# Constants of the mixers prepared earlier, the norms' power on two other engines, spare chunks in order, and other waits of query projections

## The chip, the cores and the metric

The kernel runs on one core of a Trainium2 chip. The metric is device time in microseconds (us) of one execution; lower is better. Of several executions the median counts.

## The reference: what is computed

A stack of nine sublayers works on 256 positions of width 1024 in fp32: two layers of a gated feed-forward, a mixer and another gated feed-forward (the first layer's mixer is HGRN2, a linear recurrence in chunks of 64; the second's is FOX, attention with forget gates), and then a block whose three sublayers have norms shifted, scaled and gated by a vector that is computed from a second input `c`. Its mixer, the token mixer, runs a stick-breaking attention with 8 heads and a differential attention with 4, and merges both with gates. Every mixer and feed-forward is a product with large weights (2816 columns in the feed-forward).

```python
def rmsnorm(x, g):
    x32 = x.astype(jnp.float32)
    y = x32 * lax.rsqrt(jnp.mean(x32 * x32, axis=-1, keepdims=True) + EPS)
    return (y * g.astype(jnp.float32)).astype(x.dtype)

def swiglu(h, w_in, w_out):
    gate, up = jnp.split(h @ w_in, 2, axis=-1)
    return (jax.nn.silu(gate) * up) @ w_out
...
    for layer in range(DEPTH):
        x = x + 0.5 * swiglu(rmsnorm(x, norm_g[layer, 0]), ffn_w_in[layer, 0], ffn_w_out[layer, 0])
        hn = rmsnorm(x, norm_g[layer, 1])
        if layer % N_MIXERS == 0:
            x = x + hgrn2_mixer(hn, hg_w_in[j], lbs[j], hg_out_norm_g[j], hg_w_out[j])
        else:
            x = x + fox_mixer(hn, fox_w_in[j], fox_b_f[j], fox_q_norm_g[j], fox_k_norm_g[j], fox_w_out[j])
        x = x + 0.5 * swiglu(rmsnorm(x, norm_g[layer, 2]), ffn_w_in[layer, 1], ffn_w_out[layer, 1])
...
        def sublayer(h, i, fn, resid_w):
            shift = mod[:, i, 0, None, :]
            scale = mod[:, i, 1, None, :]
            gate = mod[:, i, 2, None, :]
            u = rms_norm(h, norm_pre[l, i]) * (1.0 + scale) + shift
            return h + resid_w * gate * rms_norm(fn(u), norm_post[l, i])
...
```

## The kernel before

**Tiling.** The 256 positions are two tiles of 128, t=0 and t=1, which stay in memory on the chip as `X`. Every product is a matmul of fp32 numbers in three parts: `split` (L170 and L171) makes a high part (`H`, `w`, `uh`; a cast on ScalarE, ACT) and a low part (`L`, `q`, `ul`; a subtraction on VectorE, DVE), and `mm3` (L210 to L214) issues high times high, high times low and low times high on TensorE (PE). Weights come in chunks of 512 KB through `loadw` (L173) into 5 buffers `raw`, one DMA each or two, issued by the SyncE queue (SP); each chunk is split into two halves. `H` and `L` have 6 buffers. The next chunk's DMA starts when a `raw` buffer's last low half is made; the next casts into `H` start when PE has read the old ones.

**Stages.** Nine stages run one after another: feed-forward, HGRN2, feed-forward; feed-forward, FOX, feed-forward; ffn1, token mixer, ffn2 (the modulated three). A feed-forward projects gate and up, applies silu on ACT (L559) and a product on DVE (L564), and streams its output weights in `out_stream` (L488). There the last chunks are done first for t=0, then for t=1; what comes after t=0 (`finish`: the update of `X`, then the next stage's `norm` and its eight transposes `T`, L244) is put between the last matmuls of t=1. For t=1 the same is held as `pending` and stands in `first_pair` (L444) of the next stage: PE projects t=0 with the first weight and most of the second, then transposes t=1's norm. Some chunks are spare ones, whose parts go to buffers `w` and `q` of other pools (L188): in the modulated stages two of the output weights' last eight, and the second half of the weight that the next stage projects t=0 with last.

**Norms.** `norm` (L262) squares and sums on ACT (L271), takes mean to the power -1/2 in `rstd2` (L331: an addition on GpSimd, POOL, L333, then `pow`, L335) and scales on DVE (L277 for plain norms; for modulated ones a product with the gain in advance, L273, and then L279). `post_norm` (L348) does the same to the output of each modulated stage (L357, L360) and adds the result to `X` (L362).

**Mixers.** Each starts with constants: masks, gains and biases, loaded by DMAs on POOL's queue and prepared on DVE (HGRN2 from L613, FOX from L763 with DVE's L769 and L771, the token mixer from L971 with L985 and L987). ACT needs a table of functions per kind: silu is in one, ln and exp in another; `lnexp` (L586) loads the latter ahead of a mixer.

**Order.** PE runs in the order that the code is written in. For the mixers `weave` interleaves jobs of heads with projections: a "need" in the stream holds the projections until the named heads are done (token mixer, L1192 and L1203: the differential queries of group g wait for the stick-breaking head 3 of group g). The order of DVE, ACT, POOL and SP is made at compile time by a scheduler that estimates times; each engine then runs its list in that order. `issue_after` bounds what it may put ahead of what. So a row that waits on DVE or ACT holds all rows behind it.

Of the kernel before, what the change touches and what calls it, by code (L numbers as in the profile page):

```python
# [26 lines left out]
D = 1024  # L27
FF = 2816
P = 128
# [51 lines left out]
class Program:  # L81
# [91 lines left out]
    def loadw(self, views, shape, spare=False):  # L173
# [19 lines left out]
        for (h, l), c in zip(halves, parts):  # L193
            self.last_low = self.split(h, l, raw[c])[1]
# [67 lines left out]
    def norm(self, t, gain, shift=None):  # L262
# [11 lines left out]
        r = self.rstd2(s2)  # L274
# [62 lines left out]

    def residual(self, weight):
# [9 lines left out]
    def post_norm(self, tiles):  # L348

        def finish(t, Y):  # L350
# [137 lines left out]
    def out_stream(self, hT, w, nk, finish, last, need=None):  # L488
# [23 lines left out]

        k = 0
# [18 lines left out]
    def ffn(self, wg, wu, wo, finish):  # L532
# [22 lines left out]
        before = None  # L555
        for c0, n in SLICES:
# [23 lines left out]
            before = (c0, n)  # L580
        for n, item in enumerate(self.out_stream(lambda t, k: where[t, k], wo, FF // P, finish, self.lead)):
# [3 lines left out]

    def lnexp(self):  # L586

        es = contextlib.ExitStack()
        with contextlib.ExitStack() as a:
            if self.last_silu is not None:  # L590
                a.enter_context(self.tc.issue_after(self.last_silu.ins))
            pre = self.nc.scalar.preload_act_table_set("natural_log_exp_and_others")
        es.enter_context(self.tc.issue_after(pre.ins))
        return es
# [15 lines left out]
    def hgrn2(self, w, gain, w_out, finish):  # L610
        nc, p = self.nc, self.p

        U = self.tm([9 * P], F32R)  # L613
        raw = self.tm([9 * P])
        nc.gpsimd.dma_start(raw, p["consts"][:, C_U:C_LM])
        nc.vector.tensor_copy(U, raw)
        cm = self.tm([7 * 64 + P + 1])
        nc.gpsimd.dma_start(cm[:, :448], p["consts"][:, C_LM:C_LM + 448])
        nc.gpsimd.dma_start(cm[:, 448:576], p["consts"][:, C_WIDE:C_WIDE + P])
        nc.gpsimd.dma_start(cm[:, 576:], gain.rearrange("o d -> d o"))  # L620
# [140 lines left out]
    def fox(self, w, bf, qg, kg, w_out, finish):  # L761
        nc, p = self.nc, self.p
        cm = self.tm([256 + 16 + 2 + 1])  # L763
        nc.gpsimd.dma_start(cm[:, :272], p["consts"][:, C_FOXM:C_FOXM + 272])
        mask, gains, bias = cm[:, :256], cm[:, 272:274], cm[:, 274:275]
        for j in range(2):
            nc.gpsimd.dma_start(gains[64 * j:64 * j + 64, 0:1], qg.rearrange("o d -> d o"))
            nc.gpsimd.dma_start(gains[64 * j:64 * j + 64, 1:2], kg.rearrange("o d -> d o"))
        nc.vector.tensor_scalar(gains[:, 0:1], gains[:, 0:1], 0.125, None, op0=ALU.mult)  # L769
        sel = self.sm.tile([P, 16], F32R, name="sel", tag="sel", bufs=1)  # L770
        nc.vector.tensor_copy(sel, cm[:, 256:272])  # L771
        for j in range(3):
            nc.gpsimd.dma_start(bias[16 * j:16 * j + 16], bf.rearrange("o h -> h o"))
        zraw = self.t1([8, 16])
        nc.gpsimd.dma_start(zraw, w[:, 4 * D:].rearrange("(k p) f -> p k f", p=P))
        zw = [self.t2([8, 48], F32R) for _ in range(2)]
        self.split(*[x.rearrange("p k (j h) -> p k j h", j=3) for x in zw], zraw[:, :, None, :].to_broadcast([P, 8, 3, 16]))
# [190 lines left out]
    def token_mixer(self, lambda_init, finish):  # L968
        nc, p = self.nc, self.p
        w = p["w_in_2"][0]  # L970
        cm = self.tm([384 + 128 + 128 + 128 + 128])  # L971
        nc.gpsimd.dma_start(cm[:, :640], p["consts"][:, C_DIST:C_DIST + 640])
# [343 lines left out]
```

## Time and profile before

| | |
|---|---|
| runs | 1682.34, 1688.43 and 1692.21 us, median 1688.43 |
| profiled execution | 1683.55 us, its span 1681.7 us |
| PE busy | 1656.0 us (98% of the span), 7862 matmuls |
| DVE, ACT, POOL busy | 1138.4, 905.4 and 121.1 us |
| mean granted PE clock | 0.995 of full speed |
| chain that ended last | PE 79%, issue 11%, DVE 5%, DMA 2% |

PE is the bound nearly everywhere; what a change can move are the few places where PE stands, or runs at the lower clock. Such places are found in the list of PE's waits, in the timelines of the engines and in the tables by stretch, which give each engine's busy time and the clock granted to PE.

### The profile page before, as it was taken

The page shows a single profiled execution, that of the slowest core. Times are in us where ns is not written, and L with a number is a line of the kernel's source. Part 1 is how long each engine was busy: PE and PEld are TensorE (multiplying, and loading weights), DVE is VectorE, ACT ScalarE, POOL GpSimd, SP SyncE. Part 2 cuts the span into 40 slices and gives each one's busy share as a digit, 9 for nine tenths or more (in the row PEclk, how much of TensorE's full clock was granted, in tenths as well). Part 3 has the DMA queues.
Part 4 walks back from the last instruction along what each step waited for, and adds up shares of the span by engine and source line. Part 5 has one row for each costly group of instructions (what it writes and reads, how often), then busy time and mean ns, then how long its engine had stood idle before and what let it go on. Part 6 is the DMA issues. An engine that isn't in the chain of part 4 may idle for free.

```text
span 1681.7 us, 22653 instructions
## 1 busy us (share of the span) xinstructions
PE 1656.0 (98%) x7862; PEld 1370.1 (81%) x7862; DVE 1138.4 (68%) x2015; ACT 905.4 (54%) x1832; POOL 121.1 (7%) x218
## 2 busy tenths in 40 slices
PE   9999999999999999999999999999999999999997
PEld 7888888878888888888888888888887778778886
DVE  6885587867975688656566886575556666775553
ACT  5554476645554555547675554454545658564452
POOL 2000000020000000002211000010002000010000
PEclk9999999999999999999999999999999999999999
DMA  9885553347885588656435896576665525556651
GB/s 325 292 275 193 180 158 99 103 130 237 288 266 186 187 290 279 210 166 190 131 129 168 285 297 216 161 248 187 188 207 173 159 90 167 182 175 177 188 193 57
DMA packets 178132, 329.32 MB, mean 196 GB/s; under 512 B 13665, under 2 KB 66913, under 8 KB 178018
## 3 DMA queue, kind: packets, MB, share of 16 engines
q1 hardware_dynamic: 173328, 318.29, 59.3%
q0 software_dynamic: 4400, 9.06, 1.8%
q8 instruction: 62, 1.02, 0.3%
q10 hardware_dynamic: 290, 0.53, 0.1%
q14 instruction: 52, 0.43, 0.1%
HBM read 326.74 MB, written 1.09 MB: 195 GB/s over the span
## 4 chain that ended last, share of the span: by engine, by line
PE 79%; issue 11%; DVE 5%; DMA 2%; ACT 1%; POOL 1%; SPq 0%; DVEq 0%; POOLq 0%; ACTq 0%
PE acc L212 23%; PE acc L214 23%; PE acc L213 23%; PE T L244 2%; DVE L L171 2%; DMA raw<-in_ffn_w_in 1%; PE T L711 1%; PE acc L680 1%; PE acc L857 1%; ACT H L171 1%; POOL r L333 1%; PE T L956 0%; DVE ad L940 0%; PE T L707 0%; PE T L1063 0%
## 5 line engine op out<-in xcount | busy, mean ns | idle before, releaser
L171 DVE TENSOR_TENSOR L<-raw,H 128x512 fp32r<-128x512 f32 x1044 | 674.9, 687 | 348.6 <-ACT H L171 342.0
L171 ACT CAST H<-raw 128x512 fp32r<-128x512 f32 x1044 | 594.5, 619 | 507.9 <-PE acc L214 352.9
L212 PE MATMUL acc<-H,uh 128*128 128x512 f32 x1456 | 580.5, 399 | 0.2 <-ACT uh L171 0.2
L214 PE MATMUL acc<-H,ul 128*128 128x512 f32 x1456 | 569.1, 391 | 0.3 <-DVE ul L321 0.3
L213 PE MATMUL acc<-L,uh 128*128 128x512 f32 x1456 | 568.7, 391 | 0.0
L214 PEld LDWEIGHTS acc<-H,ul 128*128 128x128 f32 x1456 | 273.9, 188 | 59.7 <-DVE ul L321 1.0
L212 PEld LDWEIGHTS acc<-H,uh 128*128 128x128 f32 x1456 | 274.4, 188 | 54.4 <-issue 0.7
L213 PEld LDWEIGHTS acc<-L,uh 128*128 128x128 f32 x1456 | 274.5, 189 | 52.9
L212 PE MATMUL acc<-H,w 128*128 128x512 f32 x536 | 209.7, 391 | 0.0
L213 PE MATMUL acc<-L,w 128*128 128x512 f32 x536 | 208.6, 389 | 0.0
L214 PE MATMUL acc<-H,q 128*128 128x512 f32 x512 | 199.3, 389 | 0.0
L213 PEld LDWEIGHTS acc<-L,w 128*128 128x128 f32 x536 | 100.7, 188 | 20.6
L212 PEld LDWEIGHTS acc<-H,w 128*128 128x128 f32 x536 | 100.6, 188 | 20.6
L214 PEld LDWEIGHTS acc<-H,q 128*128 128x128 f32 x512 | 96.1, 188 | 19.9
L940 DVE SCALAR_TENSOR_TENSOR ad<-raw,cs,ad 128x512 f32<-128x512 f32 x126 | 94.2, 748 | 2.2
L333 POOL TENSOR_SCALAR r<-s 128x1 f32<-128x1 f32 x24 | 17.5, 728 | 701.5 <-ACT q L357 377.8
L244 PE MATMUL T<-ident,o 128*128 128x128 f32 x400 | 54.2, 276 | 6.3 <-DVE o L277 3.2
L244 PEld LDWEIGHTS T<-ident,o 128*128 128x128 f32 x400 | 46.9, 142 | 15.8 <-issue 7.4
L559 ACT ACTIVATE o<-acc 128x512 f32<-128x512 f32 (+1 forms) x72 | 39.8, 560 | 26.5 <-PE acc L214 26.2
L564 DVE TENSOR_TENSOR o<-o,acc 128x512 f32<-128x512 f32 (+1 forms) x72 | 45.1, 637 | 6.9 <-PE acc L214 4.6
L171 DVE TENSOR_TENSOR q<-T,w 128x512 fp32r<-128x512 f32 (+1 forms) x72 | 43.1, 637 | 0.0
L171 ACT CAST w<-T 128x512 fp32r<-128x512 f32 (+1 forms) x76 | 38.2, 549 | 8.3 <-PE T L244 8.3
(261 smaller groups left out, 1352.6 us busy)
## 6 DMA issues: line engine op xcount, KB each, us to landing
raw<-in_ffn_w_in SPq DMA_DIRECT2D x160, 512.0 KB, 4.9
raw<-in_ffn_w_out SPq DMA_DIRECT2D x88, 512.0 KB, 4.1
raw<-in_w_ada SPq DMA_DIRECT2D x72, 512.0 KB, 4.6
raw<-in_ffn_w_down SPq DMA_DIRECT2D x44, 512.0 KB, 3.3
raw<-in_ffn_w_gate SPq DMA_DIRECT2D x40, 512.0 KB, 3.8
raw<-in_ffn_w_up SPq DMA_DIRECT2D x40, 512.0 KB, 3.8
raw<-in_hg_w_in SPq DMA_DIRECT2D x64, 256.0 KB, 3.7
raw<-in_fox_w_in SPq DMA_DIRECT2D x64, 256.0 KB, 3.6
```

What stands on the lines that cost most here:

```text
L171: return self.nc.scalar.copy(hi, src), self.nc.vector.tensor_sub(lo, src, hi.bitcast(F32))
L212: mm(out, xh, H, start=first, stop=False)
L213: mm(out, xh, L, start=False, stop=False)
L214: mm(out, xl, H, start=False, stop=last)
L244: self.nc.tensor.transpose(T[:, j, :], src[:, (k0 + j) * P:(k0 + j + 1) * P], self.ident)
L333: self.nc.gpsimd.tensor_scalar(r, s2[:, 0:1], s2[:, 1:2], EPS, op0=ALU.add, op1=ALU.add)
L559: self.last_silu = nc.scalar.activation(s[:, :n], A[:, :n], AF.Silu)
L564: nc.vector.tensor_tensor(s[:, :n], s[:, :n], A[:, 512 - n:512], op=ALU.mult)
L680: nc.tensor.matmul(Dp.rearrange("p l c -> p (l c)"), R["lf", t][:, s, h * P:(h + 1) * P], U[:, c0:c0 + 512], start=s == 0, stop=s == 1)
L711: nc.tensor.matmul(SC[n // 3][:, n % 3, h, :].rearrange("p (b s) -> p b s", s=l), EK[h][x0 + 2 + n], q2, start=True, stop=True)
L857: nc.tensor.matmul(S[:, c], R["qz", t][:, h // 2, h % 2, :], kT[:, h // 2, :n], start=True, stop=False)
L940: nc.vector.scalar_tensor_tensor(a, raw[:, k, :], self.cs[:, k0 + k:k0 + k + 1], self.brow0 if k0 + k == 0 else a, op0=ALU.mult, op1=ALU.add)
```

## The change

Six things change.

1. The constants of the three mixers are wrapped in `preparing()`: they may start only after `quiet`, the last power before and the last `up` of the feed-forward that precedes the mixer. In the order they stand at the preceding feed-forward; before, the scheduler put them one stage earlier, next to the norm that ends it.
2. The norms and post-norms issued in the modulated stages take the power in `rstd_act`: an addition on DVE, ln and exp on ACT, and four small operations on DVE (x, and a Newton step). The twelve pairs of POOL operations go.
3. `lnexp` also loads the table of ln and exp in `fetch`, that is at the output weights of ffn1 and ffn2.
4. The spare chunks' splits in `out_stream` are held in the order of the chunks.
5. In the token mixer the differential queries of group 0 need only the start of group 1's stick-breaking, those of group 1 the head 3 of group 0; the gates' first half now needs head 3 of group 1.
6. A parameter for the descriptor memory of POOL's DMAs is set to 8192.

```diff
-            self.last_low = self.split(h, l, raw[c])[1]
+            self.last_split = self.split(h, l, raw[c])
+            self.last_low = self.last_split[1]
...
-        r = self.rstd2(s2)
+        r = self.rstd_act(s2) if self.logs else self.rstd2(s2)
...
+    def rstd_act(self, s2):
+        nc = self.nc
+        a, x, r, t, r2 = [self.ts(1, tag) for tag in ("ra", "rx", "r1", "rt", "rs1")]
+        nc.vector.tensor_scalar(a, s2[:, 0:1], EPS, None, op0=ALU.add)
+        with self.tc.issue_after(self.pre.ins):
+            nc.scalar.activation(r, s2[:, 1:2], AF.Ln, bias=a)
+            nc.scalar.activation(r, r, AF.Exp, scale=-0.5)
+        nc.vector.tensor_tensor(x, s2[:, 1:2], a, op=ALU.add)
+
+        nc.vector.scalar_tensor_tensor(t, r, r, x, op0=ALU.mult, op1=ALU.mult)
+        nc.vector.tensor_scalar(t, t, -0.5, 1.5, op0=ALU.mult, op1=ALU.add)
+        nc.vector.tensor_tensor(r2, t, r, op=ALU.mult)
+        return r2
...
-                    r = self.rstd2(s2)
+                    r = self.rstd_act(s2)
...
-                W[k] = self.loadw([w[k * P:(k + 1) * P, :].rearrange("(k p) f -> p k f", p=P)], [1, D], nk - last <= k < nk - 6)
+                spare = nk - last <= k < nk - 6
+                W[k] = self.loadw([w[k * P:(k + 1) * P, :].rearrange("(k p) f -> p k f", p=P)], [1, D], spare)
+                if spare:
+
+                    for ins in self.last_split:
+                        held.enter_context(self.tc.issue_after(ins.ins))
...
+        held.close()
         after = finish(0, Y[0])
...
+        self.quiet = [self.last_pow.ins]
...
-                nc.vector.tensor_tensor(s[:, :n], s[:, :n], A[:, 512 - n:512], op=ALU.mult)
+                self.last_up = nc.vector.tensor_tensor(s[:, :n], s[:, :n], A[:, 512 - n:512], op=ALU.mult)
...
+        self.quiet.append(self.last_up.ins)
...
+    def preparing(self):
+        es = contextlib.ExitStack()
+        for ins in self.quiet:
+            es.enter_context(self.tc.issue_after(ins))
+        return es
...
+            self.pre = self.nc.scalar.preload_act_table_set("natural_log_exp_and_others")
...
-        cm = self.tm([256 + 16 + 2 + 1])
-        nc.gpsimd.dma_start(cm[:, :272], p["consts"][:, C_FOXM:C_FOXM + 272])
+        with self.preparing():
+            cm = self.tm([256 + 16 + 2 + 1])
+            nc.gpsimd.dma_start(cm[:, :272], p["consts"][:, C_FOXM:C_FOXM + 272])
...
-                yield "need", [("sb", g, 3)]
+                yield "need", [("sb", 0, 3) if g else ("sb", 1)]
...
-                    if hf == 1:
-                        yield "need", [("da", 0, 1)]
+                    yield "need", [("da", 0, 1) if hf else ("sb", 1, 3)]
...
+                if l == 2 and i != 1:
+                    b.lnexp()
...
+            b.logs = l == 2
...
-    nc = _bacc.Bacc("TRN2", target_bir_lowering=False, num_devices=1)
+    nc = _bacc.Bacc("TRN2", target_bir_lowering=False, num_devices=1,
+                    dynamic_dma_scratch_size=8192)
```

**The place of FOX's constants.** POOL, at the end of HGRN2, where t=0's norm for the feed-forward is made (`r_3604`, `rs_3606`), before; `mod` is here the tile of FOX's constants:

```order
L764 DMA mod<-consts 128x272
L767 DMA mod<-in_fox_q_norm_g 64x1
L768 DMA mod<-in_fox_k_norm_g 64x1
L333 TENSOR_SCALAR r_3604<-s_3601 128x1
L767 DMA mod<-in_fox_q_norm_g 64x1
L768 DMA mod<-in_fox_k_norm_g 64x1
L773 DMA mod<-in_fox_b_f 16x1 x3
L335 TENSOR_TENSOR rs_3606<-r_3604,mhalf 128x1
```

And with the change (L334 and L336 are the old L333 and L335, L796 is FOX's first constant, two stages' norms further on):

```order
L334 TENSOR_SCALAR r_3604<-s_3601 128x1
L336 TENSOR_TENSOR rs_3606<-r_3604,mhalf 128x1
...
L334 TENSOR_SCALAR r_5335<-s_5332 128x1
L336 TENSOR_TENSOR rs_5337<-r_5335,mhalf 128x1
L796 DMA mod<-consts 128x272
L799 DMA mod<-in_fox_q_norm_g 64x1
```

The six small DMAs that stood between the addition and the power, or right ahead of them, are gone from there. On DVE at the same place, before:

```order
L171 TENSOR_TENSOR L<-raw,H 128x512 x3
L771 CAST sel<-mod 128x16
L171 TENSOR_TENSOR L<-raw,H 128x512 x3
L769 TENSOR_SCALAR mod<-mod 128x1
L277 SCALAR_TENSOR_TENSOR o_3599<-X_107,rs_3606,mod 128x512
```

And with the change (L278 is the old L277):

```order
L171 TENSOR_TENSOR L<-raw,H 128x512
L278 SCALAR_TENSOR_TENSOR o_3599<-X_107,rs_3606,mod 128x512
L278 SCALAR_TENSOR_TENSOR o_3600<-X_107,rs_3606,mod 128x512
L171 TENSOR_TENSOR L<-raw,H 128x512 x5
```

The norm's product moved ahead of five low halves, and the preparation of FOX's gains (L769) went elsewhere.

**The modulated norm of t=0.** DVE at the end of ffn1, where the token mixer's norm of t=0 is made, before (L273 and L279 are its two products):

```order
L273 TENSOR_TENSOR o_11848<-X_107,mod 128x512
L171 TENSOR_TENSOR L<-raw,H 128x512
L279 SCALAR_TENSOR_TENSOR o_11847<-o_11847,rs_11858,mod 128x512
L279 SCALAR_TENSOR_TENSOR o_11848<-o_11848,rs_11858,mod 128x512
L171 TENSOR_TENSOR L<-raw,H 128x512 x5
```

And with the change (L274 and L280 are the two products; L351 is the Newton step's end):

```order
L274 TENSOR_TENSOR o_11857<-X_107,mod 128x512
L343 TENSOR_SCALAR ra<-s_11858 128x1
L347 TENSOR_TENSOR rx<-s_11858,ra 128x1
L171 TENSOR_TENSOR L<-raw,H 128x512 x4
L349 SCALAR_TENSOR_TENSOR rt<-r_11867,rx 128x1
L171 TENSOR_TENSOR L<-raw,H 128x512
L350 TENSOR_SCALAR rt<-rt 128x1
L171 TENSOR_TENSOR L<-raw,H 128x512
L351 TENSOR_TENSOR rs_11869<-rt,r_11867 128x1
L280 SCALAR_TENSOR_TENSOR o_11856<-o_11856,rs_11869,mod 128x512
L280 SCALAR_TENSOR_TENSOR o_11857<-o_11857,rs_11869,mod 128x512
```

The second product stood behind one low half and stands behind six now; at the end of the token mixer the rows move in the same way.

**The tables.** ACT at the start of ffn2, where t=1's norm is made (`s_13877` its sums, `o_13955` the silu of the first gate), with the change:

```order
L272 ACTIVATE q_13881,s_13877<-X_108 128x512
L583 ACT_TABLE_LOAD
L583 ACTIVATE o_13955<-acc 128x512
L345 ACT_TABLE_LOAD
L345 ACTIVATE r_13886<-s_13877,ra 128x1
L346 ACT_TABLE_LOAD
L346 ACTIVATE r_13886<-r_13886 128x1
L171 CAST uh_114<-T 128x512 x2
```

Before, the load for silu and the silu stood there too; the two loads below and ln and exp are new, and one more load for silu follows.

## Rows read from the trace of the kernel before

**Rows 1.** Page, busy time of each engine, its share of the span and its instructions.
```profile
PE 1656.0 (98%) x7862; PEld 1370.1 (81%) x7862; DVE 1138.4 (68%) x2015; ACT 905.4 (54%) x1832; POOL 121.1 (7%) x218
```

**Rows 2.** PE's waits by line: total us, times, longest us.
```profile
PE T L244 <- DVE o L277: 3.2, 1, 3.2
PE T L244 <- DVE o L279: 2.7, 3, 1.2
PE T L1063 <- DVE w L1059: 2.0, 1, 2.0
PE acc L1093 <- ACT q L1042: 1.9, 2, 1.0
PE acc L213 <- DVE q L171: 1.4, 1, 1.4
```

**Rows 3.** Timeline, HGRN2 to feed-forward: start, us, row, idle before it <-releaser.
```profile
370.07 0.59 POOL L335 TENSOR_TENSOR rs<-r,mhalf 128x1 f32<-128x1 f32 x1
...
371.58 0.15 DVE L769 TENSOR_SCALAR mod<-mod 128x1 f32<-128x1 f32 x1 [1.59 <-DMA mod<-in_fox_q_norm_g]
371.65 1.41 DVE L277 SCALAR_TENSOR_TENSOR o<-X,rs,mod 128x512 f32<-128x512 f32 x2
```

**Rows 4.** By stretch: busy us (x instructions) of each engine, PEclk, DMA share, GB/s.
```profile
372.50:376.50 4.00, 3.96 (x14) 3.51 (x15) 2.60 (x4) 1.17 (x2) 0.00 (x0) 0.50 0.47 173
376.50:380.00 3.50, 3.50 (x13) 2.76 (x12) 2.07 (x4) 3.40 (x8) 0.00 (x0) 0.70 0.01 2
...
1347.00:1349.00 2.00, 2.00 (x9) 1.58 (x8) 1.57 (x4) 1.47 (x3) 0.00 (x0) 0.74 0.75 239
1349.00:1351.00 2.00, 2.00 (x6) 1.61 (x5) 0.70 (x2) 1.54 (x3) 0.00 (x0) 0.50 0.00 1
...
1295.00:1297.00 2.00, 1.74 (x11) 1.48 (x12) 1.24 (x3) 1.03 (x2) 0.86 (x3) 1.00 1.05 350
```

**Rows 5.** Timeline, end of ffn1, the token mixer's norm of t=0.
```profile
1278.12 1.41 DVE L279 SCALAR_TENSOR_TENSOR o<-o,rs,mod 128x512 f32<-128x512 f32 x2
1279.45 3.09 DVE L171 TENSOR_TENSOR L<-raw,H 128x512 fp32r<-128x512 f32 x5
...
1279.86 1.14 ACT L171 CAST H<-raw 128x512 fp32r<-128x512 f32 x2 [0.49 <-ACT H L171]
...
1280.70 1.03 PE L244 MATMUL T<-ident,o 128*128 128x128 f32 x8
```

**Rows 6.** Timeline, start of the token mixer, its norm of t=1.
```profile
1283.19 2.18 ACT L171 CAST H<-raw 128x512 fp32r<-128x512 f32 x4
1285.28 0.59 ACT L357 ACTIVATE q<-acc 128x512 f32<-128x512 f32 x1
...
1286.89 2.18 ACT L171 CAST w<-raw 128x512 fp32r<-128x512 f32 x4
...
1291.00 2.48 DVE L171 TENSOR_TENSOR q<-raw,w 128x512 fp32r<-128x512 f32 x4
1294.33 1.41 DVE L279 SCALAR_TENSOR_TENSOR o<-o,rs,mod 128x512 f32<-128x512 f32 x2 [0.84 <-POOL rs L335]
```

**Rows 7.** Timeline, start of ffn2, its norm of t=1.
```profile
1491.46 1.28 ACT L559 ACT_TABLE_LOAD   x1
1492.76 0.60 ACT L559 ACTIVATE o<-acc 128x512 f32<-128x512 f32 x1
...
1496.04 1.29 PE L244 MATMUL T<-ident,o 128*128 128x128 f32 x8 [1.20 <-DVE o L279]
```

**Rows 8.** By line or tile: ns of one, shortest/median/longest; chunks' DMAs, 1276 to 1290.
```profile
L985 ACT ACTIVATE le<-le x1: 207/207/207, 1214.0 to 1214.0; 128x2 f32<-128x2 f32 x1
...
L987 DVE TENSOR_TENSOR nlam<-le x1: 159/159/159, 1214.3 to 1214.3; 128x1 f32<-128x1 f32 x1
...
L333 POOL TENSOR_SCALAR r<-s x24: 296/352/2926, 5.2 to 1673.2; 128x1 f32<-128x1 f32 x24
...
DMA to landing us min/median/max: 3.0/4.4/5.8
```

More of the change, by code (lines that the diff above doesn't have):

```diff
@@ L611, in hgrn2 @@
         nc, p = self.nc, self.p
[L613 to L620, printed above, removed]
+        with self.preparing():
+            U = self.tm([9 * P], F32R)
+            raw = self.tm([9 * P])
+            nc.gpsimd.dma_start(raw, p["consts"][:, C_U:C_LM])
+            nc.vector.tensor_copy(U, raw)
+            cm = self.tm([7 * 64 + P + 1])
+            nc.gpsimd.dma_start(cm[:, :448], p["consts"][:, C_LM:C_LM + 448])
+            nc.gpsimd.dma_start(cm[:, 448:576], p["consts"][:, C_WIDE:C_WIDE + P])
+            nc.gpsimd.dma_start(cm[:, 576:], gain.rearrange("o d -> d o"))
         lm = cm[:, :448].rearrange("p (l c) -> p l c", l=7).bitcast(U32)
@@ L762, in fox @@
         nc, p = self.nc, self.p
-        cm = self.tm([256 + 16 + 2 + 1])
-        nc.gpsimd.dma_start(cm[:, :272], p["consts"][:, C_FOXM:C_FOXM + 272])
[L765 to L777, printed above, removed]
+        with self.preparing():
+            cm = self.tm([256 + 16 + 2 + 1])
+            nc.gpsimd.dma_start(cm[:, :272], p["consts"][:, C_FOXM:C_FOXM + 272])
+            mask, gains, bias = cm[:, :256], cm[:, 272:274], cm[:, 274:275]
+            for j in range(2):
+                nc.gpsimd.dma_start(gains[64 * j:64 * j + 64, 0:1], qg.rearrange("o d -> d o"))
+                nc.gpsimd.dma_start(gains[64 * j:64 * j + 64, 1:2], kg.rearrange("o d -> d o"))
+            nc.vector.tensor_scalar(gains[:, 0:1], gains[:, 0:1], 0.125, None, op0=ALU.mult)
+            sel = self.sm.tile([P, 16], F32R, name="sel", tag="sel", bufs=1)
+            nc.vector.tensor_copy(sel, cm[:, 256:272])
+            for j in range(3):
+                nc.gpsimd.dma_start(bias[16 * j:16 * j + 16], bf.rearrange("o h -> h o"))
+            zraw = self.t1([8, 16])
+            nc.gpsimd.dma_start(zraw, w[:, 4 * D:].rearrange("(k p) f -> p k f", p=P))
+            zw = [self.t2([8, 48], F32R) for _ in range(2)]
+            self.split(*[x.rearrange("p k (j h) -> p k j h", j=3) for x in zw], zraw[:, :, None, :].to_broadcast([P, 8, 3, 16]))
         cT = self.cT
@@ L981, in token_mixer @@
-        le = self.ts(2, "le")
-        for j in range(2):
-            nc.vector.tensor_tensor_reduce(lv[:, 2 * j, :], lv[:, 2 * j, :], lv[:, 2 * j + 1, :], scale=1.0, scalar=0.0,
-                                           op0=ALU.mult, op1=ALU.add, accum_out=le[:, j:j + 1])
-        nc.scalar.activation(le, le, AF.Exp)
-        nlam = self.ts(1, "nlam")
-        nc.vector.tensor_sub(nlam, le[:, 1:2], le[:, 0:1])
-        nc.vector.tensor_scalar(nlam, nlam, -lambda_init, None, op0=ALU.add)
+        with self.preparing():
+            cm = self.tm([384 + 128 + 128 + 128 + 128])
+            nc.gpsimd.dma_start(cm[:, :640], p["consts"][:, C_DIST:C_DIST + 640])
+            dist, strict, suf, none, sub = cm[:, :384], cm[:, 384:512], cm[:, 512:640], cm[:, 640:768], cm[:, 768:]
+            nc.vector.memset(none, -1.0)
+            nc.gpsimd.dma_start(sub, p["da_subln_2"].to_broadcast([P, P]))
+            nc.vector.tensor_scalar(sub, sub, 1.0 - lambda_init, None, op0=ALU.mult)
+            lv = self.t1([4, 64])
+            for j, name in enumerate(("q1", "k1", "q2", "k2")):
+                nc.gpsimd.dma_start(lv[:, j, :], p[f"da_lambda_{name}_2"].to_broadcast([P, 64]))
+            le = self.ts(2, "le")
+            for j in range(2):
+                nc.vector.tensor_tensor_reduce(lv[:, 2 * j, :], lv[:, 2 * j, :], lv[:, 2 * j + 1, :], scale=1.0, scalar=0.0,
+                                               op0=ALU.mult, op1=ALU.add, accum_out=le[:, j:j + 1])
+            nc.scalar.activation(le, le, AF.Exp)
+            nlam = self.ts(1, "nlam")
+            nc.vector.tensor_sub(nlam, le[:, 1:2], le[:, 0:1])
+            nc.vector.tensor_scalar(nlam, nlam, -lambda_init, None, op0=ALU.add)
@@ L1268, in program @@
                 if i == 1:
-                    with b.lnexp():
+                    with tc.issue_after(b.pre.ins):
                         b.token_mixer(0.8 - 0.6 * math.exp(-0.3 * 0), finish)
@@ L1278, in program @@
                 finish = finisher(b.residual(1.0), following)
-                with b.lnexp():
+                b.lnexp()
+                with tc.issue_after(b.pre.ins):
                     if l == 0:
```

14 lines of the change are left out of this document (1 added, 13 removed).

## The prediction

> **What bounds the kernel now.** PE does: it is busy 1656.0 of 1681.7 us [rows 1], and no edit touches a large matmul. So the change can pay only where PE stands or is granted the lower clock. I read three views for it: the list of PE's waits, whose five main rows make 11.2 us [rows 2]; the timelines of all engines around each of these waits, for what ended last; and the table by stretch, for the clock after the wait. One microsecond of waiting can cost two. After the 3.2 us wait for L277 the clock is 0.50 of full speed (1.2 of 2.4 GHz) for 4.0 us and 0.70 on average for the next 3.5 us; after the 2.0 us wait at L1063 it is 0.74 and 0.50 for 2.0 us each; after a wait of 1.2 us at L279 it stays at 1.00 [rows 4]. So the price behind a long wait is 4.0 x 0.50 + 3.5 x 0.30 = 3.05 us, behind the 2.0 us wait 2.0 x 0.26 + 2.0 x 0.50 = 1.5 us, behind 1.2 us nothing.
>
> **Constants (edit 1).** At the end of HGRN2 the power L335 starts only at 370.07, because FOX's DMAs were ahead of it in POOL's queue; DVE then stands 1.59 us in L769 for one of these DMAs, and the norm's product L277 is queued behind L769, until 371.65 [rows 3]. PE's transposes wait 3.2 us for it [rows 2]. With the change the power follows its addition, and L278 stands behind one low half instead of six and L769. It should be ready before PE asks. Gain: 3.2 + 3.05 = 6.25 us. If another wait of the size of L279's, 1.2 us, shows up in its place, and with it less of the clock, it is 4. The moved work (about ten small DMAs and a few DVE and ACT rows per mixer) now stands behind the last power of a feed-forward, where POOL has nothing urgent queued: POOL is busy 121 us in all [rows 1]. DVE behind a DMA could wait again at the new place, as 1.59 us in L769 [rows 3], but there PE has a whole projection ahead. I take nothing, with 1.5 us as the bound.
>
> **Queries and heads (edit 5).** The waits that this can remove are the 2.0 us at L1063, its clock price 1.5 us, and the 1.9 us at L1093 [rows 2, 4]: 5.4 us. The stretch of heads without projections around 1344 is now filled with projections of the differential queries. But these are taken from later, and a run of heads is left with less filler there; such a run costs from nothing to the 2.0 + 1.5 us that the present one costs. I take a gain of 4.5 us, between 5.4 and a loss of 1.
>
> **Spare chunks (edit 4).** PE waits 1.4 us for `q` of L171 in the output weights of the token mixer [rows 2]. The order of the chunks is now fixed, but the casts and lows before this chunk stay the same in number. I take 0, bounds -1.4 and +0.5 us (a low half more, L171 being 0.62).
>
> **Power on ACT and DVE (edit 2), norm of t=0.** POOL's two operations need 0.30 to 0.35 us (median; once 2.9) and 0.59 [rows 3, 8]. ln and exp together are about 0.4 (L985: 0.207), and a small DVE operation is 0.16 (L987) [rows 8]: an estimate of 0.4 + 0.5 = 0.9 us against 0.9. So by itself the chain costs nothing. What costs is the order. Before, L279 starts at 1278.12, behind one low half, and PE's transposes run at 1280.70 without a wait; the other five lows follow [rows 5]. Now L280 stands behind all six. The last two need casts that don't start before 1279.86, where ACT had idled 0.49 us before them for reasons that the change leaves alone [rows 5]. So: casts until 1281.0, the last low (3.09 / 5 = 0.62) until 1281.6, the end of the Newton step 1281.8, the first product (1.41 / 2) 1282.5. PE wants it at 1280.70: it waits 1.8 us, and 0.2 more for the second product. 2.0 us, and the same at the end of the token mixer.
>
> **Norm of t=1, start of the token mixer.** Before, DVE makes four `q` lows in 2.48 us while POOL does its power, waits 0.84 us for it, and L279 starts at 1294.33, its first half ready at 1295.0 [rows 6]. After, two things come later. First, ACT's list has the casts of the first spare chunk ahead of t=0's `uh` casts and those of the second right behind t=1's first square; before, all four stood behind t=1's squares. The first chunk's DMA can start when the fourth low is done, at about 1280.0, and takes 4.4 us (3.0 to 5.8) [rows 8]: 1284.4. Two casts 1.1 (half of 2.18): 1285.5. The `uh` casts 1.1: 1286.6. A square 0.6: 1287.2. Two spare casts: 1288.3. Then four casts, a square and two casts, which took from 1283.19 to 1286.89, 3.70 us [rows 6]: 1292.0. ln and exp: 1292.4; three small operations of DVE: 1292.9; the two products that make `X` 1.4: 1294.3; the norm's two products with the gain 1.3: 1295.6, with ACT's squares beside them. Second, the four `q` lows still stand ahead of the rest of the Newton step: 0.16 + 2.48, then four small rows 0.65: 1298.9. The first product 0.7: 1299.6. That is 4.6 us later than 1295.0, which includes the 2.0 us that t=0 has cost already.
>
> **The same at the start of ffn2, with tables (edits 2 and 3).** The chain is the same, 4.6 us. But ln and exp of the norm stand behind the silu of the first gate, and behind two more table loads. A load takes 1.28 us, and the next activation begins 0.02 us after its end [rows 7]. Squares end at 1491.45 + 4.6 = 1496.0; load and silu 1.9: 1497.9; load, ln, load, exp 3.0: 1500.9; three small operations and the first product 1.2: 1502.1, against 1496.04 before [rows 7]: 6.1 us. The Trainium skill ("ScalarE: Activation LUTs", section "What ACT_TABLE_LOAD costs") puts a switch at 1.28 us plus a drain of 1.38 us; by it the two loads would cost 2.8 us more and the net sum below would be +7.4. The 0.02 us in the trace speaks against the drain, so it is left out.
>
> Together 4.6 + 6.1 = 10.7 us; with DMAs of 3.0 or 5.8 us instead of 4.4 it is 7.9 or 13.5. **Clock.** PE would then wait 2.0 us twice for t=0 and, arriving 2.0 us later than before where it waited 1.2 us, 3.8 and 5.3 us for t=1. By the rows on the clock this costs between 0 and 1.5 + 3.05 + 1.5 + 3.05 = 9.1 us. The wait at the token mixer is split (PE first waits for the `q` lows of the spare chunk), so I take 1.5 there, 3.05 at ffn2, and nothing behind t=0's, which stand among full matmuls: 4.5. Total 15.2, bounds 7.9 and 22.6. At the end of the kernel the last post-norm's power is on the path, 0.2 us more. Edit 6 moves no row that PE waits for.
>
> **Sum.** -6.25 - 4.5 + 0 + 15.2 + 0.2 = +4.6 us. The profiled execution, 1683.55, becomes 1688.2. It lies 4.9 us under the median of the three runs, 1688.43; on that median the sum gives **1693.0**. With its bounds (-6.25 - 5.4 + 7.9 + 0.2 at the low end, a clock price in full at the high one without the long DMAs) this case spans 1684.9 to 1698.
>
> **Rivals.**
> *A. The norms don't get slower.* Six lows ahead of L280 cost nothing if casts come earlier than I think, and what is left of t=1's waits (1.2 us twice) goes with POOL's power. What speaks for it: one L333 took 2.926 us against a median of 0.352, beside the four `q` lows [rows 6, 8]. What speaks against: those lows stay ahead of the power in the new order too, and t=0's was not late at all. Time: -6.25 - 4.5 - 2.4 + 0.2 = -13, so 1675.5. The Trainium skill ("GPSIMD Engine Reference", section "8. Key points") says that POOL shares its SBUF interfaces with VectorE and contends with DVE instructions that have two inputs there; the long L333 agrees, and by that rule moving the power away pays. Chance 0.21.
> *B. The norms' waits bring the lower clock each time, and the DMAs are late.* 13.5 + 9.1 in place of 15.2: +12, so 1700.5, slower. It decides from the point where a wait among full matmuls gets the price of the one at L1063. For: a wait of 2.0 and one of 3.2 us did [rows 4]. Against: these stood beside small matmuls or ended a stage. Chance 0.18.
> *C. The loosened needs don't pay.* Heads without filler later in the token mixer cost 1 us instead of giving 4.5: 1698.5, slower. For: PE's total work is the same, so filler used early is missing late. Chance 0.11.
>
> **How the numbers follow.** My forecast has 0.50, of which 0.08 lie over +0.5%. About 8.4 us, 0.5%, is what a measurement can tell from no change. Rival A gives faster, 0.21; B and C give slower, 0.29, and 0.08 from the forecast: 0.37; the rest, 0.42, is the same. The cases of both signs hold most of the chance, so the likeliest one's own range, 1685 to 1698, stands beside the wide one, 1675 to 1702, which takes in A's value and B's.
>
> **What would show it.** Right: no wait for L278 after HGRN2 and clock 1.00 there; waits of PE's T for L280 of about 2 us at the ends of ffn1 and the token mixer, and of 3 to 5 us at the starts of the token mixer and ffn2, with two table loads in ACT's timeline at the latter. Wrong: transposes that run at once behind L280 (A), a clock of 0.50 behind all four waits (B), or waits in the token mixer's heads that are as long as before (C).

## The result, and the profile after

| | before | after |
|---|---|---|
| median of 7 runs each | 1687.98 us | 1697.68 us |
| lowest to highest | 1682.34 to 1692.21 | 1693.75 to 1700.15 |
| profiled execution, its span | 1683.55, 1681.7 us | 1696.75, 1695.0 us |
| PE, POOL busy | 1656.0, 121.1 us | 1663.3, 105.7 us |

The ratio is 1.0063 (95% interval 1.0043 to 1.0084): the change makes the kernel 0.63% slower. The medians differ by 9.7 us and the two profiled executions by 13.2 us; the one before lay low among its runs.

Both traces have the same matmuls, outside the token mixer in the same order, so the difference of the start times of one and the same matmul tells where time was lost. "Offset" is the start after minus the start before (inside the token mixer, where the order differs, of the matmul with the same rank):

| place | start before | start after | offset | step |
|---|---|---|---|---|
| end of HGRN2 | 364.19 | 363.92 | -0.3 | |
| feed-forward behind it | 391.31 | 384.77 | -6.5 | -6.3 |
| FOX layer's feed-forward, ahead of its first transposes | 611.10 | 604.43 | -6.7 | -0.1 |
| behind them | 623.78 | 621.53 | -2.3 | +4.4 |
| end of ffn1 | 1271.63 | 1269.01 | -2.6 | -0.4 |
| token mixer, behind t=1's norm | 1302.07 | 1307.04 | +5.0 | +7.6 |
| its heads, end of the first part | 1406.19 | 1406.79 | +0.6 | -4.4 |
| its gates | 1435.54 | 1441.88 | +6.3 | +5.8 |
| end of the token mixer | 1479.70 | 1486.17 | +6.5 | +0.1 |
| ffn2, behind t=1's norm | 1502.19 | 1518.06 | +15.9 | +9.4 |
| last matmul | 1672.00 | 1687.87 | +15.9 | 0.0 |
| end of the span | 1681.73 | 1694.98 | +13.3 | -2.6 |

PE's waits after, for [rows 2] (line, its releaser's line, total us, times, longest us):

```profile
PE T L245 <- DVE o L280: 8.9, 5, 4.0
PE acc L214 <- DVE q L171: 4.3, 3, 2.1
PE T L245 <- DVE o L588: 2.5, 2, 1.3
PE T L1145 <- ACT w L1147: 2.3, 1, 2.3
```

The 3.2 us behind L277 and the waits at L1063 and L1093 are gone; L280 (the old L279) went from 2.7 to 8.9 us, the low half `q` from 1.4 to 4.3, and the lines of L588 and L1145 are new (the old L588, L564, had waited 0.3 us). The places one by one:

**HGRN2 to feed-forward**, for [rows 3] (timeline; start, us, row). The power follows its addition at once (by the list above, it was five issues of DMAs that stood between the two before, and three that stood ahead of them), L278 runs five us earlier, and PE's transposes don't wait.

```profile
365.37 0.57 POOL L336 TENSOR_TENSOR rs<-r,mhalf 128x1 f32<-128x1 f32 x1
366.31 1.41 DVE L278 SCALAR_TENSOR_TENSOR o<-X,rs,mod 128x512 f32<-128x512 f32 x2
368.93 1.03 PE L245 MATMUL T<-ident,o 128*128 128x128 f32 x8
```

**Norm of t=0 at the end of ffn1**, for [rows 5]. Six lows ahead of L280, the casts under them until 1278.06; PE could start its transposes at 1278.2 and starts them at 1279.9:

```profile
1275.03 2.50 DVE L171 TENSOR_TENSOR L<-raw,H 128x512 fp32r<-128x512 f32 x4
1276.92 1.14 ACT L171 CAST H<-raw 128x512 fp32r<-128x512 f32 x2
1278.25 0.68 DVE L171 TENSOR_TENSOR L<-raw,H 128x512 fp32r<-128x512 f32 x1
1279.04 1.41 DVE L280 SCALAR_TENSOR_TENSOR o<-o,rs,mod 128x512 f32<-128x512 f32 x2
1279.93 1.29 PE L245 MATMUL T<-ident,o 128*128 128x128 f32 x8 [1.70 <-DVE o L280]
```

**Norm of t=1 at the start of the token mixer**, for [rows 6]. The first spare chunk's casts wait 4.62 us for their DMA with t=0's `uh` casts behind them; the post-norm's exp ends at 1290.53, but its Newton step (L349) stands on DVE behind two more lows; later PE waits for the `q` lows and then for L280:

```profile
1282.68 1.14 ACT L171 CAST w<-raw 128x512 fp32r<-128x512 f32 x2 [4.62 <-DMA raw<-in_w_in]
1283.72 1.07 ACT L171 CAST uh<-T 128x512 fp32r<-128x512 f32 x2
1290.33 0.20 ACT L346 ACTIVATE r<-r 128x1 f32<-128x1 f32 x1
1291.25 0.21 DVE L349 SCALAR_TENSOR_TENSOR rt<-r,rx 128x1 f32<-128x1 f32 x1
1295.21 0.50 PE L214 MATMUL acc<-q,uh 128*128 128x512 f32 x1 [1.89 <-DVE q L171]
1298.67 1.94 PE L245 MATMUL T<-ident,o 128*128 128x128 f32 x8 [1.25 <-DVE o L280]
```

Before, the same transposes:

```profile
1295.23 1.29 PE L244 MATMUL T<-ident,o 128*128 128x128 f32 x8 [1.24 <-DVE o L279]
```

**Norm of t=1 at the start of ffn2**, for [rows 7]. Three table loads in a row, with silu, ln and exp between them; then DVE's first row of the Newton step, idle for 2.09 us, and the transposes:

```profile
1503.85 1.28 ACT L583 ACT_TABLE_LOAD   x1
1505.14 0.60 ACT L583 ACTIVATE o<-acc 128x512 f32<-128x512 f32 x1
1505.76 1.28 ACT L345 ACT_TABLE_LOAD   x1
1507.06 0.29 ACT L345 ACTIVATE r<-s,ra 128x1 f32<-128x1 f32 x1
1507.37 1.28 ACT L346 ACT_TABLE_LOAD   x1
1508.66 0.20 ACT L346 ACTIVATE r<-r 128x1 f32<-128x1 f32 x1
1508.90 0.22 DVE L349 SCALAR_TENSOR_TENSOR rt<-r,rx 128x1 f32<-128x1 f32 x1 [2.09 <-ACT r L346]
1510.44 1.94 PE L245 MATMUL T<-ident,o 128*128 128x128 f32 x8 [4.02 <-DVE o L280]
```

**Token mixer.** The wait of 2.0 us near 1344 is gone; one of 0.4 us for ACT stays, as before. But the differential heads of group 1 now end while the gates' weights are cast, and their transposes wait for a copy of ACT that stands behind these casts:

```profile
1412.22 1.13 ACT L171 CAST H<-raw 128x512 fp32r<-128x512 f32 x2
1414.04 0.48 ACT L1147 COPY w<-T 128x384 f32<-128x384 f32 x1
1414.57 0.55 PE L1145 MATMUL T<-ident,w 128*128 128x128 f32 x3 [2.30 <-ACT w L1147]
```

**FOX layer's feed-forward.** Its first transposes wait twice for DVE's product with up:

```profile
611.35 0.66 PE L245 MATMUL T<-ident,o 128*128 128x128 f32 x4 [1.32 <-DVE o L588]
613.21 1.11 PE L245 MATMUL T<-ident,o 128*128 128x128 f32 x4 [1.20 <-DVE o L588]
```

**The clock**, for [rows 4] (by stretch; the third number from the end is PEclk): full behind HGRN2 and behind the wait of t=0, half behind that of the FOX layer's feed-forward, t=1's and the heads':

```profile
372.00:376.00 4.00, 4.00 (x20) 3.30 (x19) 4.00 (x7) 3.84 (x10) 0.00 (x0) 1.00 0.86 275
613.00:615.00 2.00, 1.79 (x7) 1.60 (x8) 2.00 (x5) 0.00 (x0) 0.00 (x0) 0.50 0.89 245
1281.00:1283.00 2.00, 2.00 (x12) 1.64 (x10) 0.00 (x0) 0.32 (x1) 0.00 (x0) 1.00 0.87 285
1298.00:1300.00 2.00, 1.33 (x7) 1.36 (x8) 1.19 (x2) 0.21 (x1) 0.52 (x1) 0.50 0.78 249
1416.00:1418.00 2.00, 2.00 (x8) 1.82 (x9) 0.59 (x1) 0.84 (x2) 0.00 (x0) 0.50 0.87 271
```

**The end.** POOL closes the program with drains. By line (ns shortest/median/longest, first and last start), before:

```profile
L1312 POOLq DRAIN  x3: 46/98/7387, 1673.6 to 1681.5; - x3
```

And after:

```profile
L1350 POOLq DRAIN  x3: 46/98/7517, 1423.3 to 1694.7; - x3
```

The long one began at 1673.6 before, beside the last power, and took 7.4 us; it begins at 1423.3 now. From the start of the last matmul to the end of the span it was 9.73 us and is 7.11.

### The profile page after: what moved, and what is told of

The parts are those of the page before. It is cut to its first block, busy times and chain, and to the rows that moved or that the text cites. A ratio compares the mean times of both kernels' runs of the same rounds, so it can differ in the third digit from the quotient of the medians.

```text
span 1695.0 us, 22728 instructions
## 1 busy us (share of the span) xinstructions
PE 1663.3 (98%) x7862; PEld 1372.6 (81%) x7862; DVE 1143.8 (67%) x2065; ACT 913.1 (54%) x1856; POOL 105.7 (6%) x198
## 5 line engine op out<-in xcount | busy, mean ns | idle before, releaser
L583 ACT ACTIVATE o<-acc 128x512 f32<-128x512 f32 (+1 forms) x72 | 39.4, 560 | 24.3 <-PE acc L215 24.2
L588 DVE TENSOR_TENSOR o<-o,acc 128x512 f32<-128x512 f32 (+1 forms) x72 | 45.2, 638 | 7.0 <-PE acc L215 5.1
L213 PE MATMUL acc<-H,o 128*128 128x512 f32 x96 | 38.9, 405 | 0.2 <-ACT o L171 0.2
```

The source lines that it names most:

```text
L213: mm(out, xh, H, start=first, stop=False)
L583: self.last_silu = nc.scalar.activation(s[:, :n], A[:, :n], AF.Silu)
L588: self.last_up = nc.vector.tensor_tensor(s[:, :n], s[:, :n], A[:, 512 - n:512], op=ALU.mult)
```

## The experiments

The theory after these traces: each edit has a place of its own; the power costs at both boundaries through the order of rows, not through ln and exp; edit 5 gives with group 0 and takes with group 1. Ratios are to the kernel before, measured beside it; microseconds are the ratio's share of its 1687. Diffs are to the kernel before, unless said otherwise; "..." marks what is left out of them.

**The power alone** (edits 2, 3 and 6 put into the kernel before).

```diff
-        r = self.rstd2(s2)
+        r = self.rstd_act(s2) if self.logs else self.rstd2(s2)
...
-                    r = self.rstd2(s2)
+                    r = self.rstd_act(s2)
...
```

> The kernel before with edits 2, 3 and 6 alone (the modulated norms' power by ln, exp and a Newton step, their table loads, the descriptor memory); constants, needs and spare chunks as before. Theory: the whole loss of the change is made here, at the two boundaries around the token mixer. The trace of the changed kernel lost 7.7 us at the first and 9.4 us at the second, so this one should be 15 to 18 us slower than before, 1.009 to 1.011, with PE waiting about 1.7 us in both transposes of t=0 and 1.9 and 1.25, then 2.05 and 4.0 us in front of those of t=1. Rival (the norms only suffer because edits 1 and 5 shift DMAs and clocks): under 8 us slower.

1.0087 (1.0067 to 1.0106): 14.7 us slower. PE's waits:

```profile
PE T L245 <- DVE o L280: 9.7, 5, 4.0
PE acc L214 <- DVE q L171: 3.2, 3, 1.4
```

So this part alone costs more than the whole change does. The rival (only DMAs and clocks that edits 1 and 5 shift) is out.

**The constants alone** (edit 1).

```diff
+        with self.preparing():
             cm = self.tm([256 + 16 + 2 + 1])
...
```

> The kernel before with edit 1 alone (the mixers' constants held until after the last power and the last up product of the feed-forward ahead). Theory: it takes away the 3.2 us wait after HGRN2 and its clock price, 6.1 us in all, and it is also the cause of the new wait of the feed-forward's transposes near 611 us (1.3 + 1.2 us and half clock, 4.2 us), since the order of VectorE's rows there moves with it: -2 us, 0.998 to 1.000. Rival (the wait near 611 us comes of another edit or of faster matmuls that meet late weights): if of another edit, no wait near 611 us and -6 us, 0.996.

0.9966 (0.9954 to 0.9978): 5.7 us faster, with no wait behind HGRN2. Near 611 us the starts of the matmuls lose only 1.0 us, not 4.2: the half of the theory that gave this edit the whole new wait is out.

**The needs alone** (edit 5).

```diff
-                yield "need", [("sb", g, 3)]
+                yield "need", [("sb", 0, 3) if g else ("sb", 1)]
...
-                    if hf == 1:
-                        yield "need", [("da", 0, 1)]
+                    yield "need", [("da", 0, 1) if hf else ("sb", 1, 3)]
```

> The kernel before with edit 5 alone (other needs of queries and gates in the token mixer). Theory: the waits near 1344 and 1368 us go (-4 to -5 us up to the middle of the mixer), and a new wait of the differential heads' transposes for ScalarE near 1412 us, with half clock, gives it back: between -1 and +3 us, 1.000 to 1.002. Rival (that wait is made by the constants or the power): -4 to -5 us, 0.997.

1.0018 (1.0003 to 1.0033): 3 us slower. The wait of the changed kernel is there with the same size, and a new one:

```profile
PE acc L213 <- ACT w L171: 2.5, 1, 2.5
PE T L1142 <- ACT w L1144: 2.3, 1, 2.3
```

The 2.5 us are the first spare chunk of the token mixer's output weights.

**Everything but the power** (edits 1, 4, 5 and 6).

The diff is to the changed kernel:

```diff
-        r = self.rstd_act(s2) if self.logs else self.rstd2(s2)
+        r = self.rstd2(s2)
...
-                    r = self.rstd_act(s2)
+                    r = self.rstd2(s2)
...
-                if l == 2 and i != 1:
-                    b.lnexp()
...
```

> The changed kernel without edits 2 and 3 (power on GpSimd everywhere, the logarithm's table loaded for the mixers alone); constants, needs and spare chunks as changed. Theory: it is the changed kernel less 15 to 17 us: 5 to 8 us faster than before by the trace's sum (-6.1 + 4.2 + 1.4 - 0.4 = -1 without the norms, so -1 to -3 if the new waits stay as they are): 0.998 to 1.000. Rival (the power on GpSimd contends with VectorE and was worth taking away): it keeps more than half of the loss, over 1.003.

0.9958 (0.9942 to 0.9975): 7.1 us faster. That lies in the 5 to 8 us with which the expectation starts, and is better than the 0.998 to 1.000 with which it ends. L280 is back at 2.7 us, as before; the heads' wait stays (2.28 us, until 1407).

**The power alone, lows held behind the norm of t=0.** The diff is to the kernel with the power alone:

```diff
...
+            if self.hold is not None:
+                es.enter_context(self.tc.issue_after(self.hold.ins))
             return cast, self.nc.vector.tensor_sub(lo, src, hi.bitcast(F32))
...
+                if self.logs and t == 0:
+                    self.hold = ins
```

> As the kernel with the power alone on ScalarE and VectorE (edits 2, 3 and 6, 14.7 us slower than before), but VectorE's low halves may only follow the second product of t=0's norm; ln, exp, the Newton step and the table loads stay. Theory (the order of the rows costs, not the operations): the waits of t=0's transposes (1.86 us twice, with the clock 3.7 and 3.8 us) go to under 0.3, the spare chunks' casts fall back behind t=1's first square, and t=1's wait at the start of the token mixer is about as before (1.2 to 1.8 us); at the start of ffn2 the two table loads still cost 2.6 to 4 us with the clock. In all 2 to 5 us slower than before, 1.001 to 1.003. Rival (ln and exp are too slow as such): at least 8 us slower, 1.005.

1.0062 (1.0041 to 1.0083): 10.5 us slower. The waits of t=0 went from 1.7 to under 0.3 us, as the theory has it. But t=1 didn't follow. The six lows now free the `raw` buffers later, the spare chunk's DMA starts later, and its casts, waiting for that DMA, hold ln of t=1's post-norm behind them on ACT (line numbers are shifted):

```profile
1292.80 1.14 ACT L173 CAST w<-raw 128x512 fp32r<-128x512 f32 x2 [1.73 <-DMA raw<-in_w_in]
1293.85 0.29 ACT L353 ACTIVATE r<-s,ra 128x1 f32<-128x1 f32 x1
...
1302.95 1.94 PE L251 MATMUL T<-ident,o 128*128 128x128 f32 x8 [2.03 <-DVE o L286]
```

My number was missed, and by its size the time is the rival's (8 us or more). What the trace shows at t=1 is a wait for a DMA ahead of ln, not slow ln and exp; at ffn2 the table loads stay and L280 is waited for as long as before this edit (4.0 us). That the order makes t=0 late is shown; that a better order of these rows would make the power free is not.

**The power alone, ffn2's norm on POOL.** To the kernel with the power alone:

```diff
-        r = self.rstd_act(s2) if self.logs else self.rstd2(s2)
+        r = self.rstd_act(s2) if self.logs and not self.long else self.rstd2(s2)
```

> As the kernel with the power alone on ScalarE and VectorE, but ffn2's norm (both tiles) takes its power on GpSimd as before, so that no table is loaded between the first gate's silu and t=1's transposes; the post-norms and the token mixer's norm keep ln and exp. Theory: of the losses 3.7 us (t=0) and 6.0 us (t=1) at the second boundary most goes: t=0's wait there vanishes and t=1's falls from 0.8 + 4.2 us to under 2; 6 to 9 us slower than before, 1.0035 to 1.0055. Rival (the post-norm's power is what makes t=1 late): less than 3 us better than the kernel with all of it.

1.0041 (1.0019 to 1.0064): 6.9 us slower, 8 us better than with all of the power. L280 falls to 5.1 us in 4 waits. At the second boundary nearly all of the loss is the norm's (by the starts of the matmuls 0.6 us are lost there in place of 9.7). This edit takes away the order of the norm's rows and its table loads together, so the share of each is not shown.

**The post-norms' power alone.** To the kernel with the power alone:

```diff
-        r = self.rstd_act(s2) if self.logs else self.rstd2(s2)
+        r = self.rstd2(s2)
```

> Edits 2, 3 and 6 for the post-norms alone; all modulated norms take their power on GpSimd as before. Theory (what costs is the norm's second product behind six low halves, and the norm's table loads): t=0's transposes don't wait at either boundary, t=1's wait about as long as before (1.4 us) or up to 1 us longer: -1 to +2 us against before, 0.9995 to 1.001, against +14.7 us with the norms too. Rival (the post-norms' ln and exp, queued behind casts that wait for DMAs, make t=1 late): t=1's transposes wait 3 us or more at the first boundary, 4 us slower or more.

0.9987 (0.9975 to 1.0000): 2 us faster, just clear of nothing. PE waits 2.5 us in three for L280, about as before, but 2.6 us for the `q` lows in place of 1.4, and by the starts of the matmuls t=1 loses 0.9 and 0.7 us at the two boundaries; the end is 2.6 us shorter. So ln and exp in the post-norms are free in the balance only; the norms' power is the loss. The kernel has edit 6 too, which is thereby out as a cause of it.

**The last post-norm alone.** To the kernel with the post-norms' power alone, whose post-norms then look at `logs`:

```diff
-                    r = self.rstd_act(s2)
+                    r = self.rstd_act(s2) if self.logs else self.rstd2(s2)
...
-            b.logs = l == 2
+            b.logs = l == 2 and i == 2
...
```

> The kernel before with one part of edit 2: only the last stage's post-norms (both tiles, the end of the kernel) take their power by ln, exp and the Newton step, with one table load more. Theory: GpSimd's last instruction is then long past, and the 7.4 us drain that stood behind its last power (end of the trace 9.7 us after the last matmul) is no longer last: the end comes 7.1 us after the last matmul, 2.3 to 2.6 us faster than before, 0.9985. Rival (the drain is hidden by the output's DMA, or is moved only): within 0.5 us of before.

1.0004 (0.9993 to 1.0015): no change that can be measured, although POOL's long drain starts at 1499.1 in its trace:

```profile
L1349 POOLq DRAIN  x3: 46/98/7387, 1499.1 to 1684.4; - x3
```

The rival holds by the time. In this trace the end comes 8.06 us after the last matmul's start, 1.7 us sooner than before. The drain was last in the trace before, but that its going shortens the runs is not shown.

**Only group 0's queries early.**

```diff
-                yield "need", [("sb", g, 3)]
+                yield "need", [("sb", 1, 3) if g else ("sb", 1)]
...
-                    if hf == 1:
-                        yield "need", [("da", 0, 1)]
+                    yield "need", [("da", 0, 1) if hf else ("sb", 1, 3)]
```

> The kernel before with half of edit 5: only the differential queries of group 0 are let go early (they need the start of the stick-breaking of group 1), those of group 1 still need its head 3. Theory: the wait of 2.0 us near 1344 us and its clock price go (-3 to -4 us in the first part of the mixer), and the new wait for ScalarE near 1412 us (2.3 us, 6.2 us with the clock) comes of group 1's queries, so it is not there: 3 to 4 us faster than before, 0.998. Rival (filler used early is missing late, whoever takes it): a wait of 2 us or more after 1400 us, and no gain.

0.9975 (0.9961 to 0.9989): 4.2 us faster; no wait at the heads' transposes after 1400. So the gain of edit 5 is group 0's and the loss group 1's.

**Edits 4 and 5.** To the kernel with the needs alone:

```diff
+                if spare:
+                    for ins in self.last_split:
+                        held.enter_context(self.tc.issue_after(ins.ins))
```

> Edits 4 and 5 alone (whole of edit 5, spare chunks in order). With edit 5 alone PE waited 2.5 and 1.1 us for the first spare chunk of the token mixer's output weights, 5.7 us in that stretch with the clock, against 2.8 us before and 2.4 us in the kernels that have both edits. Theory: fixing the order takes 3.3 us of that back; 1.0018 becomes 0.999 to 1.000. Rival (the fixed order does nothing there, the constants do): the wait stays over 3 us and the time at 1.0018.

0.9996 (0.9982 to 1.0009). The spare chunk's wait is 1.2 us in place of 2.5 and 1.1. Edit 4 repairs what edit 5 breaks there. In this run the FOX layer's feed-forward waits too, though its rows of DVE and ACT there stand in the same order as before:

```profile
PE T L245 <- DVE o L588: 2.9, 3, 1.7
```

Ahead of L588, two lows stand for their casts, and these for a weight's DMA (before, the same lows waited 0.53 us and their casts 2.13):

```profile
612.96 1.14 ACT L171 CAST H<-raw 128x512 fp32r<-128x512 f32 x2 [4.52 <-DMA raw<-in_ffn_w_in]
613.61 1.29 DVE L171 TENSOR_TENSOR L<-raw,H 128x512 fp32r<-128x512 f32 x2 [2.92 <-ACT H L171]
```

**Edits 1, 4, 6 and group 0's half of edit 5.** To the kernel with everything but the power:

```diff
-                yield "need", [("sb", 0, 3) if g else ("sb", 1)]
+                yield "need", [("sb", 1, 3) if g else ("sb", 1)]
...
-                    yield "need", [("da", 0, 1) if hf else ("sb", 1, 3)]
+                    if hf == 1:
+                        yield "need", [("da", 0, 1)]
```

> Edits 1, 4 and 6 and only the half of edit 5 that lets the queries of group 0 go early; the power stays on GpSimd and no table load is added. Theory: the gains add up: -6 us after HGRN2 (less 1 to 2 us that the constants bring back near 611 and 955 us), -4.7 us in the token mixer, and 0 to -0.5 us at the spare chunk: 8 to 10 us faster than before, 0.994 to 0.995, faster than the kernels with edit 1 alone (0.9966), half of edit 5 alone (0.9975) and everything but the power (0.9958). Rival (the parts overlap, as they did with the whole of edit 5): no better than 0.9958.

0.9936 (0.9917 to 0.9954): 10.8 us faster than before (medians 1674.03 and 1686.76 us), and faster than the change by 1.3%. The gains add up. PE's longest waits are now those of the modulated norms, as before, and those of the feed-forwards:

```profile
PE T L245 <- DVE o L280: 2.7, 3, 1.2
PE T L245 <- DVE o L588: 1.9, 3, 1.1
```

**The same with the post-norms' power.**

```diff
-                    r = self.rstd2(s2)
+                    r = self.rstd_act(s2)
...
+                if l == 2 and i != 1:
+                    b.lnexp()
...
```

> The fastest so far (edits 1, 4 and 6 and half of edit 5, 0.9936) with the post-norms' power by ln, exp and the Newton step as well; the norms keep GpSimd. Theory: the post-norms alone gave 0.9987, from the end of the kernel, where GpSimd's drain is then no longer last (2.6 us), less 0.7 to 0.9 us more in each wait of t=1: 1 to 2 us faster than that kernel, 0.992 to 0.993. Rival (the 0.0013 of the post-norms alone was chance): 0.9936 or more.

0.9935 (0.9911 to 0.9958): the same; the rival holds. The 0.0013 don't come again. In the trace the end is 2.6 us shorter (7.10 in place of 9.73), but t=1's norms lose 2.6 and 2.1 us by the starts of the matmuls; PE waits 2.8 us for `q` where it waited 1.1.

## Why the prediction was right or wrong

The median 1697.68 us lies in the range 1675 to 1702 and in the forecast's own 1685 to 1698, 4.7 us above the predicted 1693.0. It is slower by more than 0.5%, to which the text gave 0.37, against 0.42 for the same. By the starts of the matmuls, the queries came out 5.9 us worse than forecast, a place that the sum put at nothing cost 4.4, t=1's norms 1.75 more than forecast, and the end came out 2.8 better: +13.3 in the traces in place of +4.6. So it is in part luck that the median lies in the forecast's own range, 0.3 us under its upper end. By the terms of the sum:

- **Constants: -6.25 forecast, -6.3 found.** Wait and clock price as read from [rows 2 to 4]. But the execution of before was the dearest one there: the same 100 matmuls behind HGRN2 (from the start at 364.19 to that at 391.31) took 27.1 us in it, 24.3 to 26.0 in the eight other traces whose kernels keep the wait, and 20.9 in all five with edit 1. By those eight the edit is worth 3.4 to 5.1 us at this place. What they bring back at a new place was bounded at 1.5 us; in the changed kernel it is 4.4. The bound was mis-sized, but only in part by the edit: with the constants alone it was 1.0, with everything but the power 1.7, and in the run of edits 4 and 5, whose rows stand there as before, 3.7. Executions differ there by more than the 1.0 us that the edit alone costs. In that run's trace a weight's DMA is late ahead of the wait; in the changed kernel the order of DVE's rows differs as well, and the share of each stays open.
- **Queries and heads: -4.5 forecast, +1.4 found.** The step that failed is "I take a gain of 4.5 us, between 5.4 and a loss of 1"; rival C had the right size. The forecast saw that heads without filler are left, but priced them near nothing. What it didn't look at is ACT: the gates' weights, cast right behind the last early projections, stand ahead of the heads' copies.
- **Spare chunks: 0 forecast, about 0 found.** Beside edit 5 the edit is worth 3 to 4 us (1.0018 against 0.9996; 3.4 by the starts of the matmuls), which no row of before could tell.
- **Norm of t=0: 2.0 forecast at each boundary**, 2.1 found at both by the starts of the matmuls (waits of 1.70 and 1.69 for the first product, the rest between the transposes). Counting the casts that PE's reading gates, and the lows behind them, was enough.
- **Norm of t=1.** The rows came in the order of the chain. With t=0's part, 6.1 and 9.15 us with the clock were forecast, 7.6 and 9.4 found (steps of the table of starts). The transposes start later by 6.1 and 7.9 us, where 4.6 and 6.1 were forecast; the clock behind them costs 1.5 us at both, where 1.5 and 3.05 were. So at ffn2 two errors cancel, and that 9.4 is near 9.15 is luck. Two links were too short. The spare chunk's DMA: 4.4 us were taken, and from the end of the fourth low (1277.5) to the cast (1282.68) it took 5.2, at ffn2 4.9. And DVE's lows, which the sum put at nothing there: the post-norm's Newton step starts 0.7 us after its exp (1290.53 to 1291.25), at ffn2 0.9. As forecast, the loads at ffn2 come to 1.28 us each. The Trainium skill ("ScalarE: Activation LUTs", section "What ACT_TABLE_LOAD costs") adds 1.38 us of drain to a load; here the next activation starts 0.01 to 0.02 us behind each of the three, and each load as soon after the activation ahead of it, so the measured number decides.
- **End: +0.2 forecast, -2.6 found** in the trace. The chain was 0.26 us longer (L378 starts 2.45 us after the start of the last matmul, L362 2.19), but POOL's drain was not in the sum: it stands in no row of the page's engines, and I didn't read the last microseconds. What it is worth in the runs stays open, since the last post-norm alone didn't gain, and with both post-norms t=1's waits stand against it.

Rival A is out: with the power alone the kernel is 0.87% slower. The rule of the Trainium skill behind it ("GPSIMD Engine Reference", section "8. Key points", shared SBUF interfaces) fits the 2.93 us row of POOL. The forecast counted one such row; the trace before has two, one at each boundary, beside the four `q` lows:

```profile
1290.74 2.92 POOL L333 TENSOR_SCALAR r<-s 128x1 f32<-128x1 f32 x1 [2.48 <-ACT q L271]
1491.54 2.93 POOL L333 TENSOR_SCALAR r<-s 128x1 f32<-128x1 f32 x1 [3.17 <-ACT q L271]
```

But to take POOL's power away bought nothing at that place: the four `q` lows stay ahead of the small rows. Rival B didn't come in full: in the changed kernel's trace the clock stayed behind t=0's waits, as the forecast took it, and fell behind t=1's.

## What to carry to other kernels

A short operation can cost what stands ahead of it in its engine's list: before moving one to another engine, write down the rows that precede it there, what each of these waits for (here casts, buffers and a DMA), and the tables that must be changed on the way. Take a change of several edits apart: here gains of 11 us were hidden by one loss of 15. And where filler is taken to close one gap, look at all engines around the place where it is then missing.

## What the runs showed of the hardware

- The clock behind a wait is not set by the length of the wait alone. After a wait of 3.2 us behind HGRN2 the granted clock was 0.50 for 4 us before ([rows 4]), after one of 2.8 us with the power alone it was 0.50 as well, and after one of 2.9 us with edit 5 alone it was 1.00. By stretch, edit 5 alone and then the power alone:

```profile
373.00:376.00 3.00, 3.00 (x16) 2.52 (x16) 1.89 (x3) 1.50 (x3) 0.00 (x0) 1.00 0.46 175
```

```profile
376.00:379.00 3.00, 3.00 (x10) 2.52 (x9) 2.04 (x3) 1.15 (x3) 0.00 (x0) 0.50 0.36 139
```

- In HGRN2 the clock from 249 to 252 us is 1.00 in six of the fourteen profiled executions (before and after among them) and 0.50 in eight, while PE's wait ahead of it (it ends between 244.5 and 247.5 us) is 1.2 us in all fourteen; where it is 0.50, the matmuls behind it start about 3.1 us later against those ahead of it. Edits 1 and 5 alone move the time by 5.7 and 3 us, so a single profile's span says little about a change of this size. The line of before, and of edit 1 alone:

```profile
249.00:252.00 3.00, 3.00 (x17) 2.55 (x16) 2.32 (x8) 1.26 (x6) 0.90 (x2) 1.00 0.18 60
```

```profile
249.00:252.00 3.00, 3.00 (x12) 2.71 (x12) 1.74 (x6) 0.79 (x2) 0.00 (x0) 0.50 0.38 104
```
